# A hybrid decoder layer on one core: x laid out transposed by the host, and the per-layer embedding product put ahead of the normalisation

## The chip, the core and the metric

The kernel runs on one NeuronCore of a Trainium2 chip. A core has a matrix engine (TensorE, PE in the rows; PEld are its weight loads), a vector engine (DVE), a scalar engine (ScalarE, ACT), GpSimd (POOL), and SyncE (SP), whose queue issues all the DMA transfers here. Data lives in SBUF, matmul results in PSUM, which has eight banks of 128 x 512 float32. The engines run side by side, each takes its own instructions in order, and semaphores tie them together. The metric is the time on the device of one execution, in microseconds (us). Numbers that are worked out come from one profiled execution.

## The reference

One decoder layer over a sequence of 1024 tokens with 1024 features, in float32, and a final RMSNorm:

```python
h = rms_norm(x, norm_mix_g)                        # x * rsqrt(mean(x*x) + eps) * g
proj = einsum('bsd,dc->bsc', h, w_in)              # q k v z_a gk_low | cb cc xc z_c | g_a g_c
o = gla_chunked(q, k, v, gk)                       # gated linear attention, chunks of 64
y_a = (rms_norm(o) * silu(z_a)) @ w_branch_a
y_c = (cb * causal_dwconv(cc * xc) * silu(z_c)) @ w_branch_c
merged = sigmoid(g_a + b_ga) * y_a + sigmoid(g_c + b_gc) * y_c
x = x + merged @ w_out
x = x + sigmoid(rms_norm(x, norm_ple_g) @ w_ple_gate) * (p @ w_ple_proj)   # p: 1024 x 256
return rms_norm(x, norm_final_g)
```

The product `p @ w_ple_proj` (p W_pe here) depends on no other step; it is used only at the end.

## The kernel before

**Products.** Each float32 operand is split into a high and a low part: `split` casts to the high part on ScalarE and subtracts on DVE for the low part. A product is then three matmuls (`mm3`: high-high, high-low, low-high). The large products go by a Strassen scheme with seven products instead of eight: a `Cell` is one output block of 256 weight columns by 1024 tokens, and its product `k` (0 to 6) takes four kt of three matmuls of 512 columns, so 12 matmuls. The right side of product `k` is a combination of the four quarters of h, `hres[k]`, made by `build_a`: h0 and h3 are single quarters (`hq0`, `hq3`), both from the first 512 tokens; h1, h2 and h5 need sums of quarters, h4 and h6 need the others. The weights' side is loaded, split and put in a ring for each product.

**Start.** Sixteen warm-up matmuls on a zero tile run first (line 851). The loads in program order are: half the columns of W_pe (`wr_`), half the tokens of p transposed (`pr_`), a small table of vectors (`vec`), four tiles of x of 128 tokens each, the other halves of W_pe and p, and four more tiles of x (lines 864 to 873). One load of W_pe or p is 512 KB, both kt together.

**h.** `prep_x` (line 884) handles one tile of 128 tokens: ScalarE squares it and sums along the row, POOL makes the power -1/2 (`rstd_of`), DVE scales the tile, TensorE transposes eight blocks of 128 x 128 through PSUM, and DVE takes them out with the gain, `hq`.

**p W_pe.** `pe_block(b, c)` (line 897) is one block of 128 tokens by 512 columns: two kt of `mm3`, six matmuls, in one of two PSUM banks (m4, m5), copied out by ScalarE into one of four T buffers and stored to DRAM as `ped` for the end. Sixteen blocks make 96 matmuls. The first eight are among the fixed main order (`nc.side = False`); the later eight (tokens 512 on) are side work, which the planner may put between main matmuls where it likes.

**Early products.** Behind them stand sixteen products (`two_products`, line 914): products 0 and 3 of the eight gate cells, which use h0 and h3 alone. Then the layer goes on: v, q and k, z_a, conv, gates with attention woven in, branch outputs, out, and the last gate.

**Order.** All operations are noted first and put in order by a planner in the file (`Flow`). `set_dues` gives each operation the latest time that its successors allow; `put_in_order` then simulates five engines, taking at each step, among the operations that are ready on an engine, the one due first. The matmuls with `side` false keep program order; everything else is fitted in. A load is taken to have landed `LATE` (2.2 us) after its bytes would have passed at 340 KB per us. A side matmul is not planned before 0.5 us (`SIDE`) after its input from another engine. The result is a fixed order for each engine; the waits themselves are semaphores.

**Places.** Tiles of the long-lived pool `keep` take their place in SBUF when first used in that order (`Buffer.get`).

Of the kernel before, what the change touches and what calls it, by code (L numbers as in the profile page):

```python
# [162 lines left out]
class Pool:  # L163
# [60 lines left out]
class Op:  # L224
    __slots__ = ("n", "engine", "call", "args", "kw", "cost", "lat", "side", "table", "bytes", "name",
                 "preds", "succs", "left", "ready", "due", "start", "bufs")
# [10 lines left out]
class Flow:  # L237
# [5 lines left out]
    def __init__(self, tc):  # L243
        nc = tc.nc
        self.tc, self.ops, self.side, self.open = tc, [], True, []
        self.tensor, self.vector, self.scalar = Port(self, PE, nc.tensor), Port(self, DVE, nc.vector), Port(self, ACT, nc.scalar)
        self.gpsimd, self.sync = Port(self, POOL, nc.gpsimd), Port(self, SP, nc.sync)


    def note(self, engine, op, call, args, kw):  # L250
# [7 lines left out]
        o.side, o.table, o.bytes, o.bufs = self.side, 0, 0, []  # L258
# [114 lines left out]

    def put_in_order(self):
# [28 lines left out]
        while len(order) < len(ops):  # L403
# [36 lines left out]
            for b in o.bufs:  # L440
# [7 lines left out]
                b.until = max(b.until, pipe + LATE if e == SP else when + cost + (0.0 if e == PE and not o.side else o.lat))  # L448
# [5 lines left out]
    def emit(self):  # L454
        self.set_dues()
        place = lambda a: a.place() if isinstance(a, View) else a
        with self.tc.manual_schedule():
            for o in self.put_in_order():
# [7 lines left out]
LATE = 2.2  # L466


@with_exitstack
def kernel(  # L470
# [8 lines left out]
    pT: bass.AP,  # L479
    vecs: bass.AP,  # L480
# [13 lines left out]
    cp = rp = bp = sm = Pool(nc, "keep", Place(tc, "keep"))  # L494
# [19 lines left out]
    junk = cp.tile([P, D], BF16, name="junk")  # L514
# [333 lines left out]
    nc.vector.memset(f(zero), 0.0)  # L848
    warm = [psm.tile([P, 512], F32, tag=f"m{i}", name=f"warm{i}") for i in range(6)]
    nc.side = False  # L850
    for n in range(16):
# [3 lines left out]
    with phase("prep0") as pool:  # L855
        pr_ = slot(4, "h", "pTraw", (2, SEQ), F32)
        wr_ = slot(4, "l", "wperaw", (2, D), F32)
        xs = [slot(1 + n // 2, "hl"[n % 2], f"x0_{n}", (2, D), F32) for n in range(4)]
        xt = [xs[st // 2][:, st % 2, :] for st in range(8)]
# [3 lines left out]

        load(wr_[:, :, halves[0]], wpe[:, :, halves[0]])
        load(pr_[:, :, halves[0]], pT[:, :, halves[0]])
        load(vec, vecs)
        for st in range(4):
            load(xt[st], x[rows(st), :])
        load(wr_[:, :, halves[1]], wpe[:, :, halves[1]])
        load(pr_[:, :, halves[1]], pT[:, :, halves[1]])  # L870
        for st in range(4, 8):
            load(xt[st], x[rows(st), :])
        load(trim, tri)
        pth, ptl = slot(5, "h", "pThi", (2, SEQ)), slot(5, "l", "pTlo", (2, SEQ))
        wph, wpl = slot(6, "h", "wpehi", (2, D)), slot(6, "l", "wpelo", (2, D))

        def split_half(hi, lo, src, hh):
            cs = halves[hh]
            split(hi[:, :, cs], lo[:, :, cs], src[:, :, cs])

        q = [pool.tile([P, 4, HALF], F32, name=f"hq{i}") for i in range(4)]
        quad = {(0, 0): q[0], (1, 0): q[1], (1, 1): q[2], (0, 1): q[3]}

        def prep_x(st):
            ms = sm.tile([P, 1], F32, tag="ms", name=f"ms_x{st}", bufs=4)
            act(junk, xt[st], AF.Square, scale=1.0 / 32.0, accum_out=ms)
            r = rstd_of(ms, f"r_x{st}")
            nc.vector.tensor_scalar(xt[st], xt[st], r[:, 0:1], None, op0=ALU.mult)
            for kh in range(2):
                pt = pso.tile([P, 4, P], F32, tag="o", name=f"pt_x{st}_{kh}", bufs=2)  # L890
                for k in range(4):
                    kk = 4 * kh + k
                    transpose(pt[:, k, :], xt[st][:, kk * P:(kk + 1) * P])
                tt(quad[st // 4, kh][:, :, (st % 4) * P:(st % 4 + 1) * P], pt,
                   gmix[:, 4 * kh:4 * kh + 4, None].to_broadcast([P, 4, P]), op=ALU.mult)

        def pe_block(b, c):
            acc = psm.tile([P, 512], F32, tag=f"m{4 + (b + c) % 2}", name=f"pe{b}_{c}")
            nc.side = b >= 4
            for kt in range(2):  # L900
                mm3(acc, pth[:, kt, rows(b)], ptl[:, kt, rows(b)], wph[:, kt, halves[c]],
                    wpl[:, kt, halves[c]], kt == 0, kt == 1)
            nc.side = True
            t = bp.tile([P, 512], F32, tag="T", name=f"pe{b}_{c}", bufs=4)
            nc.scalar.copy(t, acc)
            store(ped[b][:, halves[c]], t)
# [7 lines left out]
        def two_products(cells):  # L914
            acc = [psm.tile([P, 512], F32, tag=f"m{n}", name=f"{c.name}X") for n, c in enumerate(cells)]
# [9 lines left out]
        split_half(wph, wpl, wr_, 0)  # L925
        split_half(pth, ptl, pr_, 0)
        split_half(wph, wpl, wr_, 1)
        for c in range(2):
            for b in range(4):
                pe_block(b, c)  # L930
        for st in range(4):
            prep_x(st)
        step(0)
        step(3)
        split_half(pth, ptl, pr_, 1)
        for st in range(4, 8):
            prep_x(st)
        two_products(pre[:4])
        for k in (1, 2):
            step(k)  # L940
        two_products(pre[4:])
        step(4)
        for c in range(2):
            for b in range(4, 8):
                pe_block(b, c)
# [596 lines left out]
def _lay_out(inp):  # L1542
# [17 lines left out]
    def quads(m):  # L1560
# [17 lines left out]
        "pT": a["p"][0, 0].T.reshape(2, 128, 1024).transpose(1, 0, 2),  # L1578
        "vecs": vecs,
# [23 lines left out]
```

## Time and profile before

| | us |
|---|---|
| median of 3 runs | 1123.13 (1121.92 to 1124.41) |
| the profiled execution | 1122.77 |
| its span, first to last instruction | 1121.0 |

| engine | busy us | share of the span | instructions |
|---|---|---|---|
| TensorE | 1104.3 | 99% | 5144 |
| DVE | 859.0 | 77% | 1377 |
| ScalarE | 586.7 | 52% | 1094 |
| POOL | 70.5 | 6% | 134 |

A timeline row gives the start from the beginning of the span, the length, the engine, the line (all operations come from one helper, so its line is the same), the operation with the tile that it writes and those that it reads, and in brackets the idle time before it with what ended that time. Lengths of matmuls overlap, since they are pipelined; the distance between two starts is what one costs the stream. The granted TensorE clock was full over the whole span (mean 0.997).

### The profile page before, as it was taken

To read this page: it belongs to the slowest core of one execution; us is meant where nothing else is said; L and a number is where in the kernel's file an instruction comes from. 1 tells how busy PE (TensorE), PEld (TensorE's weight loads), DVE (VectorE), ACT (ScalarE), POOL (GpSimd) and SP (SyncE) were. 2 spreads that over 40 slices of the span, in tenths; PEclk is the share of its full clock that TensorE was granted. 3 is DMA by queue.
4 is the path that set the end of the run, shared out by engine and by line. 5 is a ranking of instruction groups with operands and counts; after the bars stand their busy time and mean duration, and the time that the engine had idled before them with its cause. 6 is when DMAs were issued, how large, how long until landed. Compare 5 with 4: busy or idle time off the path is not lost. (4 is left out here: it accounts for less than half of the span.)

```text
span 1121.0 us, 15465 instructions
## 1 busy us (share of the span) xinstructions
PE 1104.3 (99%) x5144; PEld 915.4 (82%) x5144; DVE 859.0 (77%) x1377; ACT 586.7 (52%) x1094; POOL 70.5 (6%) x134
## 2 busy tenths in 40 slices
PE   8999999999999999999999999999999999999996
PEld 6788888888888888888888888888888888787885
DVE  6986775988885956757748677776999888879686
ACT  7766765655444333433343366766736444467553
POOL 1200000000000000000000021220000000102012
PEclk9999999999999999999999999999999999999998
DMA  9744466978993122121222599998595888778944
GB/s 342 277 168 142 133 194 187 282 231 272 318 336 112 65 85 64 49 95 47 94 57 76 173 293 316 338 294 307 183 331 170 282 263 287 294 236 284 314 163 148
DMA packets 154495, 232.66 MB, mean 208 GB/s; under 512 B 12336, under 2 KB 74032, under 8 KB 151344
## 3 DMA queue, kind: packets, MB, share of 16 engines
q1 hardware_dynamic: 154416, 231.68, 62.6%
q8 instruction: 40, 0.66, 0.2%
q14 instruction: 39, 0.32, 0.1%
HBM read 154.04 MB, written 77.59 MB: 207 GB/s over the span
## 5 line engine op out<-in xcount | busy, mean ns | idle before, releaser
L459 ACT ACTIVATE junk<-x 128x512 bf16<-128x512 f32 (+2 forms) x41 | 28.8, 703 | 21.6 <-DVE x L459 16.3
L459 POOL MEMSET t<- 128x2 f32 x8 | 0.8, 100 | 471.5 <-DVE u L459 271.0
L459 POOL TENSOR_SCALAR rg<-ms 128x1 f32<-128x1 f32 x8 | 8.1, 1007 | 259.7 <-ACT junk L459 259.7
L459 DVE TENSOR_TENSOR wt<-wt 128x512 f32<-128x512 f32 x32 | 21.7, 684 | 0.2
L459 DVE SCALAR_TENSOR_TENSOR u<-t,vec,u 128x1024 f32<-128x1024 f32 x16 | 20.4, 1278 | 0.0
L459 POOL TENSOR_TENSOR or<-or,mhalf 128x1 f32<-128x1 f32 x32 | 19.7, 618 | 2.6
L459 DVE COPY_PREDICATED aT<-trim,X 128x128 f32<-128x128 int32 x32 | 9.6, 300 | 11.1 <-PE X L459 8.6
L459 DVE TENSOR_TENSOR oT<-op,szl 128x256 f32<-128x256 f32 x32 | 13.4, 420 | 5.7 <-PE op L459 1.9
L459 ACT ACTIVATE og<-op,or 128x256 f32<-128x256 f32 x32 | 15.1, 472 | 5.1 <-POOL or L459 3.6
L459 POOL TENSOR_SCALAR or<-oms 128x1 f32<-128x1 f32 x32 | 9.8, 305 | 124.2 <-ACT junk L459 124.0
L459 DVE TENSOR_TENSOR vlo<-pt_v,vhi 128x512 fp32r<-128x512 f32 x16 | 11.0, 688 | 7.0 <-ACT vhi L459 6.9
L459 ACT ACT_TABLE_LOAD x12 | 15.4, 1283 | 0.9 <-PEq L1592 0.7
L459 ACT ACTIVATE junk<-op 128x256 bf16<-128x256 f32 x32 | 12.2, 382 | 6.8 <-PE op L459 5.9
L459 PE MATMUL op<-Sh,qkl 128*128 128x256 f32 x56 | 14.8, 284 | 0.0
L459 PE MATMUL pe<-wpehi,pThi 128*128 128x512 f32 x32 | 13.3, 414 | 1.1 <-ACT pThi L459 1.0
L459 ACT CAST vhi<-pt_v 128x512 fp32r<-128x512 f32 x16 | 9.2, 584 | 9.7 <-PE pt_v L459 8.5
L459 PE MATMUL op<-vl,aTh 128*128 128x256 f32 x64 | 13.9, 289 | 0.0
L459 PE MATMUL pe<-wpehi,pTlo 128*128 128x512 f32 x32 | 13.0, 405 | 0.5 <-DVE pTlo L459 0.5
L459 ACT CAST aTh<-aT 128x128 fp32r<-128x128 f32 x32 | 9.5, 297 | 7.4 <-DVE aT L459 7.2
L459 DVE TENSOR_TENSOR gr<-pt_g,vec 128x512 f32<-128x512 f32 x16 | 10.6, 684 | 3.2 <-DMA gd<-gr 2.4
L459 DVE TENSOR_TENSOR Sl<-S,Sh 128x256 fp32r<-128x256 f32 x28 | 11.8, 421 | 1.6 <-ACT Sh L459 1.3
L459 PEld LDWEIGHTS X<-qkl 128*128 128x128 f32 x64 | 11.3, 189 | 1.9
(3228 smaller groups left out, 4195.1 us busy)
## 6 DMA issues: line engine op xcount, KB each, us to landing
qkl<-qkd SPq DMA_DIRECT2D x32, 320.0 KB, 5.1
x<-in_x_dram SPq DMA_DIRECT2D x16, 512.0 KB, 6.0
wt<-in_wb_dram SPq DMA_DIRECT2D x8, 1024.0 KB, 6.4
wtd<-wt SPq DMA_DIRECT2D x32, 256.0 KB, 4.2
vl<-vd SPq DMA_DIRECT2D x32, 256.0 KB, 5.0
uq<-ud SPq DMA_DIRECT2D x5, 1024.0 KB, 6.6
oq<-od SPq DMA_DIRECT2D x5, 1024.0 KB, 7.0
ped<-pe SPq DMA_DIRECT2D x16, 256.0 KB, 3.1
```

The source lines that it names most:

```text
L459: o.call(*[place(a) for a in o.args], **{k: place(a) for k, a in o.kw.items()})
```

## The change

- The host hands in x a second time, transposed (`xT`), as eight kt of 128 features by 1024 tokens. The four quarters `hq` are loaded from it directly; the eight tiles of x are no longer loaded here, nor transposed.
- `scale_h(i)` takes the place of `prep_x` for one half of the tokens: ScalarE squares the eight kt (four instructions of 1024 columns), DVE adds them up to two, eight float32 matmuls of one column against `ones` sum over the features into PSUM, DVE adds EPS, POOL takes the power -1/2 of four columns, DVE copies it out four times 128 wide, four transposes bring it along the columns, and eight `scalar_tensor_tensor` scale `hq` with the gain.
- All sixteen blocks of p W_pe stand ahead of the early products in the main order, over six banks; the first four go kt by kt. Their copies alternate between ScalarE and DVE. The early products use other banks in turn.
- The loads of W_pe and p are one kt each (256 KB), p and W_pe by turns; these loads and the splits of W_pe and p are due 8 us earlier for the planner (`hurry`).
- In the first 30 us of the plan a load counts as landed 0.8 us after its bytes, not 2.2 us.
- Nine warm-up matmuls instead of sixteen.
- `lay_out` gives the tiles of `keep` their places before the first instruction, `mhalf` first and then from the largest down; `junk` is half as wide.

```diff
+    def lay_out(self, first):
+        tags = sorted(self.tags.values(), key=lambda t: (t.name != first, -t.buffers[0].size * (1 + (t.buffers[0].dtype != BF16))))
+        for t in tags:
+            b = t.buffers[0]
+            for n in range(len(t.free)):
+                if not any(c.real is not None for c in t.buffers):
+                    self.opened().tile([P, b.size], b.dtype, tag=f"{t.name}_{n}", name=f"at_{t.name}_{n}", bufs=1)
...
+        for o in self.ops:
+            o.due -= o.hurry
...
-                q.ready = max(q.ready, (pipe + LATE if e == SP else when + cost + q.preds[n])
+                q.ready = max(q.ready, (pipe + (LATE if when > START else 0.8) if e == SP else when + cost + q.preds[n])
...
+START = 30.0
...
-    for n in range(16):
+    for n in range(9):
         mm(warm[n % 6], zero[:, 0:P], zero, start=True, stop=True)
...
+        q = [pool.tile([P, 4, HALF], F32, name=f"hq{i}") for i in range(4)]
+        quad = [(0, 0), (1, 0), (1, 1), (0, 1)]
...
+        def get_x(i):
+            for n in (0, 3) if i == 0 else (1, 2):
+                for kp in range(0, 4, 2):
+                    kk = 4 * quad[n][1] + kp
+                    load(q[n][:, kp:kp + 2, :], xT[:, kk:kk + 2, halves[i]])
+
+        nc.hurry = 8.0
+        for kt in range(2):
+            load(pr_[:, kt, halves[0]], pT[:, kt, halves[0]])
+            load(wr_[:, kt, halves[0]], wpe[:, kt, halves[0]])
+        for kt in range(2):
+            load(wr_[:, kt, halves[1]], wpe[:, kt, halves[1]])
+        nc.hurry = 0.0
+        get_x(0)
+        load(vec, vecs)
+        for kt in range(2):
+            load(pr_[:, kt, halves[1]], pT[:, kt, halves[1]])
+        get_x(1)
...
+        def scale_h(i):
+            both = (0, 3) if i == 0 else (1, 2)
+            acc = slot(1, "hl"[i], f"sq{i}", (4, 512), F32)
+            for j, (n, kp) in enumerate((n, kp) for n in both for kp in (0, 2)):
+                d = acc[:, 0:2, :] if j == 0 else acc[:, 2:4, :] if j % 2 else slot(2, "hl"[i], f"sr{i}", (4, 512), F32)[:, 0:2, :]
+                act(d, q[n][:, kp:kp + 2, :], AF.Square, scale=1.0 / 32.0)
+                if j:
+                    tt(acc[:, 0:2, :], acc[:, 0:2, :], d, op=ALU.add)
+            sums = pso.tile([P, 4, P], F32, tag="o", name=f"ms{i}", bufs=2)
+            for s in range(4):
+                for kt in range(2):
+                    mm(sums[:, s, 0:1], acc[:, kt, s * P:(s + 1) * P], ones, start=kt == 0, stop=kt == 1)
+            r = sm.tile([P, 4], F32, tag="rx", name=f"r_x{i}", bufs=2)
+            nc.vector.tensor_scalar(r, sums[:, :, 0], EPS, None, op0=ALU.add)
+            nc.gpsimd.tensor_tensor(r, r, mhalf[:, 0:1].to_broadcast([P, 4]), op=ALU.pow)
+            rb = bp.tile([P, 4, P], F32, tag="u2", name=f"rb{i}", bufs=2)
+            nc.vector.tensor_copy(rb, r[:, :, None].to_broadcast([P, 4, P]))
+            rt = pso.tile([P, 4, P], F32, tag="o", name=f"rt{i}", bufs=2)
+            for s in range(4):
+                transpose(rt[:, s, :], rb[:, s, :])
+            rt = rt.rearrange("p s t -> p (s t)")
+            for n in both:
+                for k in range(4):
+                    kk = 4 * quad[n][1] + k
+                    stt(q[n][:, k, :], q[n][:, k, :], gmix[:, kk:kk + 1], rt, op0=ALU.mult, op1=ALU.mult)
+
+        at = [0]
+        BANKS = (0, 1, 2, 3, 4, 5, 0, 1, 2, 3, 4, 5, 0, 1, 2, 3)
+
+        def pe_blocks(bs, c, by_kt=False):
+            acc = []
+            for b in bs:
+                n = BANKS[at[0]] if at[0] < len(BANKS) else 4 + at[0] % 2
+                acc.append(psm.tile([P, 512], F32, tag=f"m{n}", name=f"pe{b}_{c}"))
+                at[0] += 1
+            todo = [(b, kt) for kt in range(2) for b in bs] if by_kt else [(b, kt) for b in bs for kt in range(2)]
+            for b, kt in todo:
+                nc.side = at[0] > len(BANKS)
+                mm3(acc[b - bs[0]], pth[:, kt, rows(b)], ptl[:, kt, rows(b)], wph[:, kt, halves[c]],
                     wpl[:, kt, halves[c]], kt == 0, kt == 1)
+                nc.side = True
+                if kt == 1:
+                    t = bp.tile([P, 512], F32, tag="T", name=f"pe{b}_{c}", bufs=4)
+                    (nc.vector.tensor_copy if b % 2 else nc.scalar.copy)(t, acc[b - bs[0]])
+                    store(ped[b][:, halves[c]], t)
...
+        nc.hurry = 8.0
+        for kt in range(2):
+            split(pth[:, kt, halves[0]], ptl[:, kt, halves[0]], pr_[:, kt, halves[0]])
+            split(wph[:, kt, halves[0]], wpl[:, kt, halves[0]], wr_[:, kt, halves[0]])
+        nc.hurry = 0.0
+        pe_blocks(range(0, 4), 0, True)
         split_half(wph, wpl, wr_, 1)
...
+        pe_blocks(range(0, 4), 1)
+        split_half(pth, ptl, pr_, 1)
+        pe_blocks(range(4, 8), 0)
+        pe_blocks(range(4, 8), 1)
+        scale_h(0)
         step(0)
         step(3)
...
+        two_products(pre[:4], (4, 5, 0, 1))
+        scale_h(1)
         for k in (1, 2):
             step(k)
+        two_products(pre[4:], (2, 3, 4, 5))
         step(4)
```

## Rows read from the trace of the kernel before

**Rows 1.** The page, busy time of each engine: us (share of span) xinstructions.

```profile
PE 1104.3 (99%) x5144; PEld 915.4 (82%) x5144; DVE 859.0 (77%) x1377; ACT 586.7 (52%) x1094; POOL 70.5 (6%) x134
```

**Rows 2.** TensorE waits behind 100 us: us in total, times, longest.

```profile
PE out0V L459 <- ACT out0hi L459: 0.7, 1, 0.7
```

**Rows 3.** Timeline of TensorE near 60 us: start, length, engine, operation, idle before.

```profile
60.19 0.39 PE L459 MATMUL ga3pX<-h3hi,ga3phi 128*128 128x512 f32 x1
60.42 0.39 PE L459 MATMUL ga3pX<-h3lo,ga3phi 128*128 128x512 f32 x1
```

**Rows 4.** Timeline of TensorE, the start.

```profile
1.44 3.78 PE L459 MATMUL warm<-zero 128*128 128x512 f32 x8 [1.44 <-DVE zero L459]
...
8.15 0.50 PE L459 MATMUL pe<-wpehi,pThi 128*128 128x512 f32 x1 [1.03 <-ACT pThi L459]
8.49 0.39 PE L459 MATMUL pe<-wpelo,pThi 128*128 128x512 f32 x1
9.41 0.50 PE L459 MATMUL pe<-wpehi,pTlo 128*128 128x512 f32 x1 [0.53 <-DVE pTlo L459]
```

**Rows 5.** Timeline of TensorE, two later stops and what ended them.

```profile
25.07 0.50 PE L459 MATMUL ga0pX<-h0lo,ga0phi 128*128 128x512 f32 x1 [0.84 <-DVE h0lo L459]
...
34.85 0.66 PE L459 MATMUL pt_x<-ident,x 128*128 128x128 f32 x4 [0.56 <-DVE hq L459]
```

**Rows 6.** First load issue; DMA queue view, 40 slices of the first 40 us.

```profile
0.72 0.69 SPq L459 DMA_DIRECT2D wperaw<-in_wpe_dram  x1
...
GB/s 0 0 223 330 320 311 330 367 401 426 396 396 399 397 399 412 383 369 354 367 373 412 389 401 412 375 315 324 365 385 387 391 334 393 389 318 90 297 279 193
```

**Rows 7.** Timeline of ScalarE, the start.

```profile
4.62 1.05 ACT L459 CAST wpehi<-wperaw 128x1024 fp32r<-128x1024 f32 x1 [2.62 <-DMA wperaw<-in_wpe_dram]
7.05 1.04 ACT L459 CAST pThi<-pTraw 128x1024 fp32r<-128x1024 f32 x1 [1.39 <-DMA pTraw<-in_pT_dram]
...
16.28 0.62 ACT L459 CAST ga0phi<-ga0praw 128x512 fp32r<-128x512 f32 x1
```

**Rows 8.** Timeline of DVE, 26 to 32 us.

```profile
26.07 2.35 DVE L459 TENSOR_TENSOR h3lo<-hq,h3hi 128x1024 fp32r<-128x1024 f32 x2
...
30.15 0.69 DVE L459 TENSOR_TENSOR gc0plo<-gc0praw,gc0phi 128x512 fp32r<-128x512 f32 x1
31.60 0.78 DVE L459 TENSOR_SCALAR x<-x,r_x 128x1024 f32<-128x1024 f32 x1 [0.77 <-POOL r_x L459]
```

**Rows 9.** Timeline of TensorE, four transposes and the next matmuls.

```profile
20.66 0.60 PE L459 MATMUL pt_x<-ident,x 128*128 128x128 f32 x4
21.01 0.47 PE L459 MATMUL pe<-wpehi,pTlo 128*128 128x512 f32 x1
21.32 0.39 PE L459 MATMUL pe<-wpehi,pThi 128*128 128x512 f32 x1
```

**Rows 10.** Timeline of TensorE in the attention stage, a float32 matmul and a transpose.

```profile
646.35 0.38 PE L459 MATMUL X<-qkl 128*128 128x128 f32 x2
646.57 0.27 PE L459 MATMUL X<-ident,qkl 128*128 128x128 f32 x1
646.60 0.48 PE L459 MATMUL ga0V<-h5hi,ga0hi 128*128 128x512 f32 x1
```

**Rows 11.** Windows, 40 to 60 us: busy us (xinstructions) of each engine, granted clock.

```profile
40.00:60.00 20.00, 19.98 (x92) 15.88 (x91) 18.80 (x20) 14.47 (x22) 0.64 (x2) 1.00 0.66 232
```

**Rows 12.** Timeline of POOL, 26 to 32 us.

```profile
27.47 3.44 POOL L459 TENSOR_SCALAR r_x<-ms_x 128x1 f32<-128x1 f32 x1 [10.42 <-ACT junk L459]
31.00 0.57 POOL L459 TENSOR_TENSOR r_x<-r_x,mhalf 128x1 f32<-128x1 f32 x1
```

**Rows 13.** Tile S, one kind: duration ns min/median/max, first and last start.

```profile
L459 DVE SCALAR_TENSOR_TENSOR S<-S,dds,X x24: 471/474/476, 654.9 to 755.8; 128x256 f32<-128x256 f32 x24
```

**Rows 14.** Tensor ped, first 30 us: issues (ns) and landing.

```profile
L459 SPq DMA_DIRECT2D ped<-pe x2: 326/328/330, 11.7 to 13.2; - x2
...
DMA to landing us min/median/max: 4.7/5.1/5.5
```

More of the change, by code (lines that the diff above doesn't have):

```diff
@@ L225 @@
     __slots__ = ("n", "engine", "call", "args", "kw", "cost", "lat", "side", "table", "bytes", "name",
-                 "preds", "succs", "left", "ready", "due", "start", "bufs")
+                 "preds", "succs", "left", "ready", "due", "start", "bufs", "hurry")
 class Port:
@@ L257, in note @@
         o.n, o.engine, o.call, o.args, o.kw = len(self.ops), engine, call, args, kw
-        o.side, o.table, o.bytes, o.bufs = self.side, 0, 0, []
+        o.side, o.table, o.bytes, o.bufs, o.hurry = self.side, 0, 0, [], self.hurry
         label = lambda v: v.buf.name if isinstance(v, View) else "in"
@@ L447, in put_in_order @@
                     b.ends[e] = when + cost
-                b.until = max(b.until, pipe + LATE if e == SP else when + cost + (0.0 if e == PE and not o.side else o.lat))
+                b.until = max(b.until, pipe + (LATE if when > START else 0.8) if e == SP else when + cost + (0.0 if e == PE and not o.side else o.lat))
                 if not b.left:
@@ L456, in emit @@
         place = lambda a: a.place() if isinstance(a, View) else a
+        order = self.put_in_order()
+        self.keep.lay_out("mhalf")
         with self.tc.manual_schedule():
-            for o in self.put_in_order():
+            for o in order:
                 o.call(*[place(a) for a in o.args], **{k: place(a) for k, a in o.kw.items()})
@@ L479 @@
     pT: bass.AP,
+    xT: bass.AP,
     vecs: bass.AP,
@@ L848 @@
     nc.vector.memset(f(zero), 0.0)
+    ones = sm.tile([P, 1], F32, name="ones")
+    nc.gpsimd.memset(ones, 1.0)
     warm = [psm.tile([P, 512], F32, tag=f"m{i}", name=f"warm{i}") for i in range(6)]
     nc.side = False
-    for n in range(16):
+    for n in range(9):
         mm(warm[n % 6], zero[:, 0:P], zero, start=True, stop=True)
@@ L862 @@
                for m, bias, dst in (("ga", bga, gad), ("gc", bgc, gcd)) for c in range(4)]
[L864 to L873, printed above, removed]
+        q = [pool.tile([P, 4, HALF], F32, name=f"hq{i}") for i in range(4)]
@@ L874 @@
+        quad = [(0, 0), (1, 0), (1, 1), (0, 1)]
         pth, ptl = slot(5, "h", "pThi", (2, SEQ)), slot(5, "l", "pTlo", (2, SEQ))
         wph, wpl = slot(6, "h", "wpehi", (2, D)), slot(6, "l", "wpelo", (2, D))
-        def split_half(hi, lo, src, hh):
[L878 to L890, printed above, removed]
-                for k in range(4):
[L892 to L901, printed above, removed]
-                    wpl[:, kt, halves[c]], kt == 0, kt == 1)
[L903 to L906, printed above, removed]
+        def get_x(i):
[3 more added lines that the diff above has]
+                    load(q[n][:, kp:kp + 2, :], xT[:, kk:kk + 2, halves[i]])
@@ new lines @@
+        nc.hurry = 8.0
[10 more added lines that the diff above has]
+        get_x(1)
+        load(trim, tri)
+        def split_half(hi, lo, src, hh):
+            nc.hurry = 8.0
+            for kt in range(2):
+                cs = halves[hh]
+                split(hi[:, kt, cs], lo[:, kt, cs], src[:, kt, cs])
+            nc.hurry = 0.0
@@ L912, in step, with two_products @@
             hres[k] = hb[k]
-        def two_products(cells):
-            acc = [psm.tile([P, 512], F32, tag=f"m{n}", name=f"{c.name}X") for n, c in enumerate(cells)]
+        def two_products(cells, banks):
+            acc = [psm.tile([P, 512], F32, tag=f"m{n}", name=f"{c.name}X") for n, c in zip(banks, cells)]
             for c, X in zip(cells, acc):
@@ L1578, in _lay_out @@
         "pT": a["p"][0, 0].T.reshape(2, 128, 1024).transpose(1, 0, 2),
+        "xT": a["x"][0].T.reshape(8, 128, 1024).transpose(1, 0, 2),
         "vecs": vecs,
```

26 lines of the change are left out of this document (6 added, 20 removed).

## Prediction

> **What bounds the kernel now.** I read the page's busy shares first: TensorE is busy 99% of the span [rows 1]. The reader should see there that shortening other engines buys nothing by itself: the time is TensorE's own instructions plus the places where it stands. So I then read its waits and its timeline. Behind 100 us the longest entry in the list of waits is 0.7 us [rows 2]; in the steady part the product matmuls follow each other every 0.227 us [rows 3]. What the change touches lies ahead of that stream, so the question is how much earlier the stream gets going, and how many instructions leave it.
>
> The start of before: warm-up matmuls from 1.44 us, then idle until pThi, first p W_pe matmul at 8.15 [rows 4]. After it a gap is the distance between two starts less 0.23: 8.49 to 9.41 gives 0.69, where the row itself says 0.53 of idle, so a restart costs 0.16 more than the idle time shown. The two other stops, 0.84 for h0lo and 0.56 for a transpose [rows 5], are then 1.00 and 0.72. Together 2.4 us of standing after 8.15.
>
> **The change, part by part.**
>
> *The first matmul.* Before, ScalarE waits for the first load, 512 KB of W_pe issued at 0.72, until 4.62, and for the second, 512 KB of p, until 7.05; its cast of 1024 columns takes 1.04, and TensorE starts at 8.15 [rows 4, 6, 7]. After, these loads are cut in four of 256 KB, p and W_pe by turns, and the first matmul needs two of them: as many bytes as the one load that had landed by 4.62. A cast of 512 columns takes 0.62 [rows 7], and 0.06 passes between the cast's end at 8.09 and the matmul at 8.15. So 4.62 + 0.62 + 0.06 = 5.30. The warm-up is cut to nine: the first eight take 3.78 us from 1.44 [rows 4], so the ninth ends near 5.5. I take 5.4: 2.75 us earlier (1.9 if the pair lands as late as 5.5; 3.1 if warm-up and landing both let it start at 5.05).
>
> *Its second matmul* needs wpelo, one DVE subtraction of 512 columns, 0.69 [rows 8], behind the cast: a gap of about 0.45. The second kt is needed eleven matmuls later, at 8.4; its two loads land one and two 256 KB transfers later, 0.8 us each at 330 KB per us [rows 6], by 6.2, so its parts are there by 7.6. No stall.
>
> *Work taken from TensorE.* The 64 transposes of x go. Four of them push the stream back by 0.35 (20.66 to 21.01), and the next matmul by 0.31 - 0.23 = 0.08 [rows 9]: 0.43 for four, 16 x 0.43 = 6.9 us, all in the continuous stream and so on the path. New on TensorE: eight transposes of the broadcast rstd, 2 x 0.43 = 0.9; and sixteen float32 matmuls of one column against ones. Nothing in the trace is one column wide. The nearest row is the float32 matmul of 128 columns, which is two instructions, 646.35 to 646.57, 0.11 each [rows 10]; 32 x 0.11 = 3.5, with 0.3 for the stream resumed 3.8. From below, an instruction can start 0.03 behind a transpose (646.57 to 646.60): 32 x 0.03 = 1.0. I take 3.8, because the 128 x 128 to be loaded as weights is the same. Net -6.9 + 0.9 + 3.8 = -2.2 us (to -5.0 with the lower end).
>
> *The order.* All 96 matmuls of p W_pe now run first: 5.4 + 0.45 + 96 x 0.227 = 27.6 us [rows 3], plus the first half's sums and transposes, 2.3: the first product wants h0 at about 30. Moving the blocks costs no TensorE time; but before, the later 48 of them were filler while DVE was busy 18.8 of 20 us [rows 11]. Is that filler missed? The sixteen early products read h0 and h3 alone, both made of the first half of the rows of x, so the second half is not wanted for another 16 x 12 x 0.227 = 43.6 us. In this time DVE has some twelve wlo (12 x 0.69 = 8.3), the second half's three adds (1.18 each, half of 2.35 [rows 8]) and eight scalings (0.74, below), 9.5, and for h3, h1, h2 and h4 about 16 x 1.18 = 19: 37 of 44 us. Cover enough.
>
> *h0 in time.* Six loads of 256 KB and four of 512 KB go ahead of it, 3.7 MB at 330 KB per us from 2.0 us, with 1 us of lag as for the first load: 14.2 us [rows 6, 7]. Then, each from its nearest row: last square 1.05 (as the cast of 1024), add 1.18, 16.4; eight sums 1.8; rstd 0.2 and 0.57 on DVE and POOL [rows 12]; broadcast copy 0.4, four transposes 0.5, 19.9; four scalings (a scalar_tensor_tensor of 256 columns takes 0.47 [rows 13]; 0.27 for 256 more, half of 1.18 - 0.69 and a little, gives 0.74), 22.9; last cast and subtraction 2.2: 25.1. DVE's other work in the stretch (six copies of blocks, two wlo, 0.69 each at most) can push that to 28 or so. Slack 2 to 5 us. Where it gives: the planner lines sums and transposes up between matmuls, and a transpose lined up earlier than its input is there holds TensorE, as at 34.85 [rows 5]. I allow 0.5 for each half and 0.5 at the first product: 1.5 + 0.45 = 1.95 of standing against 2.4, -0.45 (from -1.95 without these to +1.5).
>
> *The rest.* Squares, adds, scalings and casts run on ScalarE and DVE beside TensorE, at nothing while the slack holds. Loads' precedence and the shorter delay in the planner make the first matmul early; counted there. Tiles' places in order of size change addresses alone: the products already stand at 0.227 us, so I book nothing, and within 1 us either way for the later order, which the planner works out anew (nearest row: one late wait of 0.7 [rows 2]).
>
> *Sum.* -2.75 - 2.2 - 0.45 = -5.4. The profiled span of 1121.0 becomes 1115.6; 1.8 lie around it in that execution (1122.77), and the median 1123.13 is 0.36 above that: about **1117.7 us**. With the bounds: 1114.5 to 1120.0.
>
> **Rivals.**
>
> *The loads come no sooner.* If the four 256 KB transfers share the queue and land together, the first pair is there only after 1 MB, when p landed before: cast from 7.05 to 7.67, start at 7.7, a gain of 0.4 instead of 2.75: 1120.0. For it: the second load of before came 2.4 us after the first, not the 1.5 of its bytes. Against it: the first did land by 4.62 with others issued behind it [rows 6, 7].
>
> *POOL held off by DVE.* Each half's rstd has a pow on POOL between DVE steps. At 27.47 a one-column POOL instruction took 3.44, against 0.57 for the pow behind it, while DVE ran subtractions without a pause; it ended at 30.91, when DVE had gone idle [rows 8, 12]. If pow stands like that in both halves, beyond the planner's margin of 0.5, TensorE, in order, stands 2 x (3.44 - 0.57 - 0.5) = 4.7 at the transposes instead of the 1.0 allowed there: 1121.4, no change. Against it: DVE's own broadcast copy waits for pow, so DVE goes idle after at most the few instructions queued between. [...]
>
> *Blocks' copies stand for their buffers: slower.* The sixteen block copies share four T buffers, each freed when its store has landed. Copy 0.62 (as the cast), issue 0.33 and landing 5.1 (the two in the first 30 us took 4.7 and 5.5 [rows 14]) make a turn of 6.05 per four blocks, which TensorE computes in 5.45. Three turns: 1.8 us late, inside the slack. But the copies stand in order on ScalarE and DVE ahead of the squares and scalings of h0, and all filler is spent: at a landing L the chain is late by 3 x (L - 4.5). The gain without the 1.5 allowed is 6.9, the slack about 4: from 10.9 us late, L = 8.1, the kernel is slower than before. At L = 10 it stands 16.5 - 4 = 12.5: 1123.1 - 6.9 + 12.5 = 1128.7. Against it: neither early store took that long.
>
> **How the numbers follow.** Forecast 0.66, 1117.7 (own range 1114.5 to 1120.0, all of it faster). Loads no sooner 0.12, 1120.0, faster. POOL 0.13, 1121.4, no change. T buffers 0.09, slower. A measurement of this kernel can tell about 0.2%, 2.2 us, from no change. So faster 0.78, same 0.13, slower 0.09. The range takes the forecast's bounds, the second case and the third: 1114.3 to 1121.6.
>
> **What would show it.** First p W_pe matmul near 5.4 us; no gap over 0.5 us until the products; the 32 instructions of the sums 0.03 to 0.11 apart; first product near 30 us; behind it the rows of before, 5 us earlier. Wrong, if the first product stands for h0lo by more than 3 us, if ScalarE waits for ped stores, if pow takes over 2 us with TensorE waiting behind it, or if the waits behind 100 us grow.

## The result, and the profile after

The changed kernel takes **1113.45 us** (1113.04 to 1114.01), the one before 1123.77 on the same chip: a ratio of 0.9909 [0.9892, 0.9927]. That is faster, as forecast, but 4.25 us below the forecast of 1117.7 and 0.85 below the range. The executions of before spread from 1121.9 to 1125.2, and its profiled one is among the short ones, so medians gain 10.3 us and profiled executions 8.9 (1122.77 to 1113.84); what follows is accounted in the profiles.

The page of after, span and busy time of each engine, as in [rows 1]:

```profile
span 1112.1 us, 15377 instructions
PE 1098.6 (99%) x5113; PEld 912.6 (82%) x5113; DVE 865.6 (78%) x1391; ACT 582.8 (52%) x1082; POOL 59.5 (5%) x121
```

TensorE's timeline in after: the start, the first half's sums and transposes, and the first products. It answers to [rows 4, 5, 9].

```profile
1.44 4.21 PE L474 MATMUL warm<-zero 128*128 128x512 f32 x9 [1.44 <-DVE zero L474]
5.45 0.71 PE L474 MATMUL pe<-wpehi,pThi 128*128 128x512 f32 x1
5.95 0.63 PE L474 MATMUL pe<-wpelo,pThi 128*128 128x512 f32 x1
6.38 0.63 PE L474 MATMUL pe<-wpehi,pTlo 128*128 128x512 f32 x1
6.80 0.45 PE L474 MATMUL pe<-wpehi,pThi 128*128 128x512 f32 x1
7.09 0.39 PE L474 MATMUL pe<-wpelo,pThi 128*128 128x512 f32 x1
...
19.10 1.84 PE L474 MATMUL ms<-ones,sq 128*128 128x1 f32 x16
20.80 0.49 PE L474 MATMUL pe<-wpehi,pThi 128*128 128x512 f32 x1
21.13 0.40 PE L474 MATMUL pe<-wpelo,pThi 128*128 128x512 f32 x1
...
23.22 0.60 PE L474 MATMUL rt<-ident,rb 128*128 128x128 f32 x4
23.58 0.48 PE L474 MATMUL pe<-wpelo,pThi 128*128 128x512 f32 x1
23.90 0.39 PE L474 MATMUL pe<-wpehi,pTlo 128*128 128x512 f32 x1
...
30.27 0.39 PE L474 MATMUL ga0pX<-h0hi,ga0phi 128*128 128x512 f32 x1
...
31.86 0.39 PE L474 MATMUL ga0pX<-h0lo,ga0phi 128*128 128x512 f32 x1
```

There is no idle time in brackets after 1.44 us: the stops of before between 8 and 35 us have no successor. One of them [rows 5] does not show, since its idle time is short; the distance is 0.51, so 0.29 too much:

```profile
32.01 0.39 PE L459 MATMUL ga2pX<-h0lo,ga2phi 128*128 128x512 f32 x1
32.52 1.06 PE L459 MATMUL pt_x<-ident,x 128*128 128x128 f32 x8
```

Three other things are to be seen in after. The first matmuls stand 0.50, 0.43, 0.42 and 0.29 apart, about double the usual distance at first. Sixteen one-column instructions take 20.80 - 19.10 = 1.70 us. And behind the sums the matmuls stand 0.23 apart for a while, where they stood 0.227 before them.

What fed TensorE in after: ScalarE's first casts and one copy of a block, DVE's second half of h0lo, and POOL's two powers.

```profile
4.03 0.62 ACT L474 CAST wpehi<-wperaw 128x512 fp32r<-128x512 f32 x1 [2.03 <-DMA wperaw<-in_wpe_dram]
4.68 0.62 ACT L474 CAST pThi<-pTraw 128x512 fp32r<-128x512 f32 x1
...
17.80 0.59 ACT L474 COPY pe<-pe 128x512 f32<-128x512 f32 x1 [0.35 <-DMA ped<-pe]
```

```profile
22.67 0.43 DVE L474 COPY rb<-r_x 128x512 f32<-128x512 f32 x1 [0.92 <-POOL r_x L474]
...
29.18 1.21 DVE L474 TENSOR_TENSOR h0lo<-hq,h0hi 128x1024 fp32r<-128x1024 f32 x1
```

```profile
21.30 1.34 POOL L474 TENSOR_TENSOR r_x<-r_x,mhalf 128x4 f32<-128x4 f32 x1 [19.98 <-DVE r_x L474]
47.12 1.02 POOL L474 TENSOR_TENSOR r_x<-r_x,mhalf 128x4 f32<-128x4 f32 x1 [24.48 <-DVE r_x L474]
```

**The account.** A fixed mark is the first q product, behind all that was changed; its rows in before and in after:

```profile
178.00 0.39 PE L459 MATMUL q0X<-h0hi,q0hi 128*128 128x512 f32 x1
```

```profile
168.81 0.39 PE L474 MATMUL q0X<-h0hi,q0hi 128*128 128x512 f32 x1
```

So 9.2 us are gained ahead of it (0.3 are lost behind it). A second profile of each kernel has 177.53 and 168.43, so the mark moves by some 0.4 us from one execution to the next. Distances between TensorE's starts, after less before, summed by what stands there:

| us | |
|---|---|
| first block earlier, 8.15 to 5.45 | -2.7 |
| 64 transposes of x | -6.1 |
| 32 instructions of the sums | +3.4 |
| eight transposes of rstd | +0.7 |
| stops of before that are gone (0.69, 1.01, 0.29, 0.73, and 0.24 at 106 us) | -2.9 |
| first matmuls at double distance | +0.7 |
| the rest: the first matmul behind a stop or a group of transposes, 0.31 to 0.34 instead of 0.227; gaps of up to 0.2 between products; 0.1 in all for matmuls at 0.229 to 0.237 | -2.3 |

### The profile page after: what moved, and what is told of

It is laid out like the page before. It is cut to its first block, busy times and chain, and to the rows that moved or that the text cites. A ratio compares the mean times of both kernels' runs of the same rounds, so it can differ in the third digit from the quotient of the medians.

```text
span 1112.1 us, 15377 instructions
## 1 busy us (share of the span) xinstructions
PE 1098.6 (99%) x5113; PEld 912.6 (82%) x5113; DVE 865.6 (78%) x1391; ACT 582.8 (52%) x1082; POOL 59.5 (5%) x121
## 4 chain that ended last, share of the span: by engine, by line
PE 93%; DVE 3%; DMA 2%; issue 1%; ACT 0%; POOL 0%; SPq 0%; POOLq 0%; DVEq 0%; ACTq 0%
PE op L474 2%; PE pe L474 2%; PE X L474 2%; DMA qkl<-qkd 1%; PE ga2Y L474 1%; PE ga3Y L474 1%; PE gc1Y L474 1%; PE gc0Y L474 1%; PE v2Y L474 1%; PE gt0Y L474 1%; PE v1Y L474 1%; PE v3Y L474 1%; PE v0Y L474 1%; PE out3Y L474 1%; PE out0Y L474 1%; PE gt1Y L474 1%
## 5 line engine op out<-in xcount | busy, mean ns | idle before, releaser
L474 ACT ACTIVATE junk<-x 128x512 bf16<-128x512 f32 (+1 forms) x33 | 20.3, 616 | 20.6 <-DVE x L474 15.6
L474 PE MATMUL X<-qkl 128*128 128x128 f32 x64 | 12.5, 276 | 0.7 <-DMA qkl<-qkd 0.5
L474 PE MATMUL X<-vl,keh 128*128 128x256 f32 x56 | 12.9, 312 | 0.0
L474 PE MATMUL pe<-wpelo,pThi 128*128 128x512 f32 x32 | 12.8, 400 | 0.0
```

The source lines that it names most:

```text
L474: o.call(*[place(a) for a in o.args], **{k: place(a) for k, a in o.kw.items()})
```

## The experiments

The open question was where the unforeseen 3.5 us of the profiles came from: out of the work removed (a transpose costs more than its own time: the first matmul behind a group stands 0.31 instead of 0.227 [rows 9]) or out of the order (the early blocks cover what TensorE used to stand for). Edits are to the changed kernel unless said otherwise.

**The changed kernel again**, and the p W_pe part alone: blocks, loads, planner and places as changed, x as in before (`prep_x` with its 64 transposes).

> The changed kernel again, beside the runs that it is compared with. Theory S (the stream's own account): of 9.2 us that the changed kernel is ahead when the q products begin, 2.7 are the earlier first matmul, 2.9 stops of TensorE that are gone, 2.7 transposes less sums, and about 0.9 slower matmuls behind each break. It gives 1113 to 1114 us, 0.991 of before. Theory F (the forecast's terms, 5.4 us) gives 1118.

> The other part alone: blocks first over six banks, cut loads with precedence, nine warm-up matmuls, planner and places as changed; x still loaded in tiles, scaled and transposed on TensorE. S: the earlier first matmul (2.7) and some of the stops (1 to 2.5) go, the 64 transposes stay: 3.5 to 5.5 us ahead of before, 1118.5 to 1120.5 us. R: everything but the 2.7 of transposes, 6.5 us ahead, 1117. A missing filler (h0 late, blocks all spent): the first product stands for h0lo by several us and the kernel is no faster than before.

They took 1113.62, ratio 0.9888 [0.9868, 0.9908], and 1116.13, 0.9908 [0.9888, 0.9928], beside 1125.83 for before. The x part adds 2.5 us only. The second kernel came out better than theory S had it, and nearer to R. With the transposes still in it, the second kernel has no stop between 1.44 us and its first q product:

```profile
171.78 0.39 PE L474 MATMUL q0X<-h0hi,q0hi 128*128 128x512 f32 x1
```

That is 6.2 us ahead of before, of which the start explains 2.5 (its first block stands at 5.68). So it is the order over six banks, with the start, that took the stops away.

**The later eight blocks as side work behind the products again**, over two banks.

```diff
-        pe_blocks(range(4, 8), 0)
-        pe_blocks(range(4, 8), 1)
         scale_h(0)
...
         step(4)
+        pe_blocks(range(4, 8), 0)
+        pe_blocks(range(4, 8), 1)
```

> The changed kernel with the later eight blocks of p W_pe put back as filler behind the early products (two banks, side work), everything else as changed. If the filler is not missed (forecast and S): h0 is then wanted 11 us earlier, near 19 us, and can't be there before 28: TensorE stands some 6 to 9 us at the first product, or the planner pulls the blocks forward and nothing changes; 1113 to 1122. If moving the blocks was worth nothing: 1113 to 1114, and the blocks stand ahead of the first product anyway.

It took 1125.38, ratio 1.0 [0.9985, 1.0015]: 11.8 us over the changed kernel, the whole gain, and more than either expectation. Its timeline of TensorE:

```profile
17.21 0.50 PE L474 MATMUL pe<-wpehi,pThi 128*128 128x512 f32 x1 [2.89 <-ACT pe L474]
...
28.05 0.51 PE L474 MATMUL ga0pX<-h0hi,ga0phi 128*128 128x512 f32 x1 [2.57 <-ACT h0hi L474]
...
29.43 0.79 PE L474 MATMUL ga0pX<-h0lo,ga0phi 128*128 128x512 f32 x1 [0.87 <-DVE h0lo L474]
```

TensorE stands 6.3 us in three stops: the first for one of the two banks, which ScalarE's late copy frees, the other two for h0, with no block left to do meanwhile. The stops are not the whole price. Behind the first one the granted clock falls (in a window, the third number from the end; here 0.50), and matmuls stand 0.43 apart:

```profile
20.00:25.00 5.00, 5.00 (x15) 4.02 (x16) 3.00 (x6) 1.66 (x3) 1.34 (x1) 0.50 1.06 381
```

At the first q product (181.22) this kernel is 12.4 us behind the changed one: 6.9 in the stops with their restarts, 4.8 at the lower clock. The edit puts back the two banks together with the old order, and no run takes them apart, so what the order is worth without the banks is not shown.

**The x part alone** on the kernel before, tiles placed by first use as there.

> The x part alone on the kernel before: x loaded transposed and scaled in place; order, loads of p and W_pe, warm-up and planner as before. S: 2.7 us of transposes less sums, the stops at 32 to 34 us (1.0 us) and most of the slower matmuls go, the first matmul stays near 8.2: 4 to 5.5 us ahead of before, 1118 to 1120 us. F: 2.2 us of work alone, 1121. Rival R (the surplus of 3.8 us over the forecast comes from the planner's new order and the tiles' places): at most 2.7 us, 1121.

1139.96, ratio 1.0122 [1.0098, 1.0147]: much slower, which nothing in any of my reasons explained. The products stood 0.230 to 0.232 apart in every stage. The places of tiles came under suspicion; see the runs on places below.

**The start: uncut loads, the old plan, sixteen warm-ups.** First, the first half of p and all of W_pe in loads of 512 KB, W_pe first:

```diff
-        for kt in range(2):
-            load(pr_[:, kt, halves[0]], pT[:, kt, halves[0]])
-            load(wr_[:, kt, halves[0]], wpe[:, kt, halves[0]])
+        load(wr_[:, :, halves[0]], wpe[:, :, halves[0]])
+        load(pr_[:, :, halves[0]], pT[:, :, halves[0]])
...
```

> The changed kernel with W_pe and p loaded 512 KB at a time, W_pe first, as before. S: the first matmul falls back to 7.5 to 8.2 us, 2 to 2.7 us slower than the changed kernel. If h0 is what sets the first product at 30 us: 0 to 0.5 slower.

1117.35, ratio 0.9937 [0.992, 0.9953], 3.7 us over the changed kernel. TensorE's first block there:

```profile
8.61 0.59 PE L474 MATMUL pe<-wpehi,pThi 128*128 128x512 f32 x1 [2.98 <-ACT pThi L474]
```

Again the clock falls behind the stop, so not all of the 3.7 is the later start (3.2 in the profile):

```profile
9.00:10.00 1.00, 1.00 (x4) 0.57 (x3) 0.97 (x3) 0.82 (x3) 0.00 (x0) 0.50 1.02 383
```

Second, no precedence and the long delay in the plan (`START = -1.0`, `o.due -= 0.0`):

> The changed kernel without the planner's part: no 8 us of precedence for the loads and splits of p and W_pe, and a load counted as landed 2.2 us after its bytes also in the first 30 us. S: places of a few instructions differ; if precedence is what makes the first matmul early, loads of x go ahead and it starts 0.5 to 2.5 us later (1114 to 1116). R: most of the surplus of 3.8 us is lost, 1117.

1114.2, 0.9913 [0.9898, 0.9927], first block at 5.55. So the loads, cut and by turns, make the first matmul early, and the planner's two edits are worth nothing that shows. Third, `range(16)` for the warm-ups:

> The changed kernel with sixteen warm-up matmuls instead of nine. In the changed kernel the first three p W_pe matmuls are 0.43 to 0.50 us apart, twice the later distance. With sixteen, the warm-up ends near 7.1 us instead of 5.4, and the first matmuls run at 0.23: 1.1 us slower if the slow matmuls are gone with it, 1.7 if not. If the early start is worth less than it looks (h0 sets the first product anyway): no slower.

1114.22, 0.9913 [0.9898, 0.9927]: 0.6 more than the changed kernel's 1113.62 on another chip; in the profiles its first q product is 1.1 later (169.92). The first block waits until 7.31, and no matmul then stands at double distance. But with nine warm-ups that happens too; the second profile of the changed kernel:

```profile
5.36 0.50 PE L474 MATMUL pe<-wpehi,pThi 128*128 128x512 f32 x1
5.70 0.40 PE L474 MATMUL pe<-wpelo,pThi 128*128 128x512 f32 x1
6.08 0.51 PE L474 MATMUL pe<-wpehi,pTlo 128*128 128x512 f32 x1
6.43 0.40 PE L474 MATMUL pe<-wpehi,pThi 128*128 128x512 f32 x1
```

So nine warm-ups don't bring the double distance by themselves; it differs from one execution to the next. The clock's row has 1.00 in both, but the trace of after holds no record of the clock before 6.91 us, where the double distance ends, and the second one none before 4.94; 0.43 is the distance that the run with uncut loads shows at a granted clock of 0.50.

**Work on TensorE.** Four unread transposes behind each block put the 64 back, and nothing else; then the sums with their two kt added on DVE first, 8 instead of 16 matmuls:

```diff
+            tt(acc[:, 0, :], acc[:, 0, :], acc[:, 1, :], op=ALU.add)
             for s in range(4):
-                for kt in range(2):
-                    mm(sums[:, s, 0:1], acc[:, kt, s * P:(s + 1) * P], ones, start=kt == 0, stop=kt == 1)
+                mm(sums[:, s, 0:1], acc[:, 0, s * P:(s + 1) * P], ones, start=True, stop=True)
```

> The changed kernel with 64 transposes of 128 x 128 put in again, four behind each block of p W_pe, with nothing reading them: what they cost by themselves. The forecast's price: 16 x 0.43 = 6.9 us slower. S: 7.2 for the transposes and the matmul behind each group, and matmuls at 0.230 to 0.232 instead of 0.227 for some twenty behind each: 7.5 to 8.3. Less than 5 if part of them was hidden.

> The changed kernel with the two remaining kt of the squares added on DVE, so that eight one-column float32 matmuls do instead of sixteen. S: 16 instructions less, 1.7 us faster, at 0.6 us of DVE in each half: 1111.5 to 1112.5.

The first took 1121.01, ratio 0.9969 [0.9957, 0.9982], 7.4 more than the changed kernel, and its first q product is 7.36 later: 5.67 in the transposes, 1.23 in the block matmuls behind them, the rest in products. The forecast had 6.9. Its timeline, one group of four:

```profile
11.34 0.39 PE L474 MATMUL pe<-wpehi,pTlo 128*128 128x512 f32 x1
11.57 0.60 PE L474 MATMUL pt_d<-ident 128*128 128x128 f32 x4
11.92 0.48 PE L474 MATMUL pe<-wpehi,pThi 128*128 128x512 f32 x1
12.24 0.39 PE L474 MATMUL pe<-wpelo,pThi 128*128 128x512 f32 x1
```

The second took **1112.03**, ratio 0.9881 [0.9866, 0.9896]: 1.6 less than the changed kernel's 1113.62 on another chip, the fastest of all. Eight instructions in place of sixteen take 0.81 us instead of 1.70 (its own rows), and DVE's added operation hides:

```profile
19.92 0.95 PE L474 MATMUL ms<-ones,sq 128*128 128x1 f32 x8
20.73 0.48 PE L474 MATMUL pe<-wpehi,pTlo 128*128 128x512 f32 x1
```

**The sums twice**: a second pair of the same matmuls into a column that nobody reads.

> The changed kernel with the sixteen one-column float32 matmuls made twice (the second time into a column that nobody reads): 32 instructions more on TensorE, and rstd later by 1.7 us in each half. By the trace of after, 16 take 1.70 us: 3.4 us slower, plus what h0 then comes late: h0lo's second half was there at 30.3, when the first product began at 30.27, so up to 1.7 more if the stream does not move with it. By the forecast's lower bound (0.03 each): 1.0.

1122.18, ratio 0.9982 [0.9971, 0.9994]: 8.6 more, where the instructions themselves cost 4.8 and the expectation was at most 5.1 (its profile, at 1124.50, is longer than its median). Its windows (start:end, length, busy us with instructions of TensorE, its loads, DVE, ScalarE, POOL, then granted clock) and its timeline behind the first sums:

```profile
20.00:30.00 10.00, 10.00 (x43) 8.54 (x43) 4.07 (x9) 2.87 (x6) 1.34 (x1) 0.66 0.88 292
50.00:60.00 10.00, 10.00 (x45) 8.62 (x46) 3.39 (x7) 1.21 (x2) 1.41 (x1) 0.66 0.55 201
```

```profile
18.66 4.39 PE L474 MATMUL ms<-ones,sq 128*128 128x1 f32 x32
22.91 0.77 PE L474 MATMUL pe<-wpehi,pThi 128*128 128x512 f32 x1
23.48 0.63 PE L474 MATMUL pe<-wpelo,pThi 128*128 128x512 f32 x1
23.91 0.63 PE L474 MATMUL pe<-wpehi,pTlo 128*128 128x512 f32 x1
```

The 32 instructions of one column took 4.25 (18.66 to 22.91), not twice 1.70; the granted clock was 0.66 in the mean of each of those windows, and matmuls behind them stood 0.43 apart, as at 0.50 in the run with the late blocks. Block and product matmuls together are 4.7 us longer than in after, most of it here. Around sixteen in a row, in the changed kernel, the clock's row has 1.00.

**Three buffers for the copies of blocks** instead of four (`t = ev(f"pe{b}_{c}")`), for the third rival.

> The changed kernel with the block copies going through three buffers (shared with the early products' copies) instead of four. By the forecast's rival of the copies: a turn of 6.05 us per three blocks, which TensorE computes in 4.1, so the chain is 5 x 1.95 = 10 us late and TensorE stands 5 to 10 us: 1118 to 1124. If stores land faster than 5.1 us: under 2 us.

1117.46, ratio 0.9937 [0.9922, 0.9951]: 3.8 more. Its profile, of the longest of four executions (1120.20), has two stops that cost 1.0 and 1.7, and a granted clock of 0.51 between 45 and 50 us behind the second. Both stops wait for DVE, for a copy of a block and for an addition; the longest wait of a copy for a store is one of 0.43 on ScalarE. So fewer buffers cost time, in a plan that comes out differently, but the wait for stores that the rival is about isn't seen.

**Places.** First, the changed kernel without `lay_out`:

```diff
-        self.keep.lay_out("mhalf")
```

> The changed kernel with the tiles' places taken in order of first use, as before. S and the forecast: addresses cost nothing, within 0.5 us of the changed kernel, product matmuls 0.227 us apart. R: 1 to 4 us slower.

1131.77, ratio 1.0065 [1.0049, 1.0082]: 18 us over the changed kernel. Its first product starts at 30.01, as early as in the changed one; its products then stand 0.230 to 0.232 apart to the end. Listed from the built kernels, all places in `keep` are multiples of 32 bytes, and TensorE's large operands start at 32 modulo 64 in before and after; in this one and in the x part alone they are mixed, since the tile `ones`, one column wide, pushes what is placed behind it by 32 bytes. The theory formed then: what counts is whether the two operands of a matmul start alike modulo 64. A pad of one column in front of everything big (all at 0), against a pad behind the resident tiles, in front of the streamed weights (weights at 0, h at 32):

```diff
+                    if t.name == first:
+                        self.opened().tile([P, 1], F32, tag="pada", name="at_pada", bufs=1)
```

```diff
+                    if t.name == "u2" and n == 0:
+                        self.opened().tile([P, 1], F32, tag="pada", name="at_pada", bufs=1)
```

> The changed kernel with every large tile moved by 32 bytes, so that all operands of TensorE start on a multiple of 64. Theory U (the mixture of starts is what costs): as the changed kernel, 1113 to 1114.5, matmuls 0.227 us apart. Theory V (a start on a multiple of 64 is the slow one): 0.231 or more and 1131 us or above. Theory W (the sizes' order itself, which puts neighbours together, is what helps, not the start): 1113.5.

> The changed kernel with the resident operand (h, u, o, the weights of the last stages) 32 bytes past a multiple of 64 and the ring of the other operand on it. U: mixed between the two operands of one matmul, 0.231, 1130 us; if only a mixture from one matmul to the next costs: 1113.5. V: half of the reads slow, 1120 to 1130. W: 1113.5.

1113.73, ratio 0.9903 [0.9888, 0.9918], against 1138.8, 1.0127 [1.0112, 1.0142]. Windows of 100 us in the middle, the first of all shifted, the second of weights shifted:

```profile
400.00:500.00 100.00, 100.00 (x443) 82.84 (x442) 61.48 (x91) 37.95 (x66) 0.20 (x2) 1.00 0.21 67
```

```profile
400.00:500.00 100.00, 100.00 (x430) 80.51 (x429) 62.13 (x93) 34.56 (x60) 0.20 (x2) 1.00 0.23 75
```

Same work, busy 100% and clock 1.00 in both, and 3% fewer matmuls done in the second. Both operands at 0 or both at 32 gives 0.227 a product matmul, one of each 0.233; over some 4400 of them that makes the difference of 25 us. U had named 1130, near the run without places; but there only about half of the matmuls have operands that differ. With the starts listed beside each matmul, the trace of that run agrees: 0.233 where they differ, 0.229 to 0.231 where they are alike (why not 0.227 stays open). In the changed kernel itself 32 matmuls have operands that differ, and they stand 0.234 apart.

**The x part alone with the places laid out:**

> The x part alone on the kernel before, now with the tiles' places in order of size, so that all operands of TensorE start alike. By the trace of the run without places, where the products were 0.231 to 0.232 us apart over the whole span (4400 x 0.0045 = 20 us): 1139.9 - 20 = 1120 us. By the difference between the changed kernel and the run of the other part alone (2.5 us): 1121.

1121.93, ratio 0.9983 [0.9967, 0.9999]; the 18 us of the run without places are gone, but there is no gain ahead of the first q product (178.24). Three stops of TensorE, on the pe banks and on h0, and a granted clock of 0.76 between 25 and 30 us behind them, ate the transposes' time:

```profile
15.76 0.50 PE L471 MATMUL pe<-wpehi,pThi 128*128 128x512 f32 x1 [1.20 <-ACT pe L471]
...
24.96 0.50 PE L471 MATMUL ga0pX<-h0hi,ga0phi 128*128 128x512 f32 x1 [1.14 <-ACT h0hi L471]
...
26.33 0.50 PE L471 MATMUL ga0pX<-h0lo,ga0phi 128*128 128x512 f32 x1 [0.87 <-DVE h0lo L471]
```

**The start alone and the order alone**, both on the kernel before with places laid out: cut loads and nine warm-ups; all sixteen blocks first over six banks.

> The kernel before with the first loads cut in 256 KB, p and W_pe by turns, and nine warm-up matmuls; blocks in the order of before; tiles' places as in the changed kernel. The first matmul comes 2.5 us earlier, but h0 is ready when it was (25 us), so the early start should turn into a longer stop before the first product: 0 to 1 us ahead of before. If an early start is worth its time anywhere: 2.5.

> The kernel before with all sixteen blocks of p W_pe ahead of h over six banks, and nothing else of the change but the tiles' places (operands start alike). If the order removes the stops: the 1.0 us for h0lo, the 0.3 and 0.7 at 32 to 34 us and the small ones go, the first matmul stays at 8.2, 64 transposes stay: 2.5 to 4 us ahead of before. If the stops go with the early start: 0 to 1.

1121.93, 0.9973 [0.9958, 0.9987], and 1120.83, 0.9964 [0.9947, 0.9981]. At the first q product the start alone is 1.0 us ahead of before, the order alone 2.8, both together (the p W_pe part) 6.2. With the old order the early start turns into stops, first for the second kt of p, then at h0:

```profile
7.37 0.50 PE L471 MATMUL pe<-wpehi,pThi 128*128 128x512 f32 x1 [0.84 <-ACT pThi L471]
...
25.11 0.50 PE L471 MATMUL ga0pX<-h0lo,ga0phi 128*128 128x512 f32 x1 [1.43 <-DVE h0lo L471]
```

**The kernel before again**, for the spread of its times.

> The kernel before, profiled once more. Its runs spread over 4 us (1122 to 1126), those of the changed kernel over 1.3. If its start is what differs (stops at the hand-over from the blocks to h0, or a clock that falls in them): the difference to the first profile lies in the first 100 us. If not: it is spread over the span, or lies in the late waits at 950 to 1035 us.

1121.73, span 1120.0, with the same stops, all some 0.4 us earlier. It is a short one again, so a long one was not caught. But each execution has its mean granted clock on record. Of 65 executions of before beside the other runs (one of 2314 us left out), the 31 at 0.997 or more have a median of 1123.4 us, the 15 at 0.995 or less one of 1126.3; the changed kernel's eight are all at 0.997 or 0.998. So the longer ones go with a lower clock. That it falls behind the stops, as in the runs above, fits, but isn't shown.

## Why the prediction was right in sign and too small

**First matmul: right.** 5.45 for 5.4; cast at 4.03, the second at 4.68. Its inner reason was half wrong: precedence and delay in the plan, which I counted in, are worth nothing that shows; the loads, cut and by turns, do it alone.

**The gap for wpelo: wrong in kind, small.** No gap of 0.45; instead four matmuls at up to double distance, 0.74 in all; that a lower clock made them isn't shown. In the second profile it is 0.39, and the first distances there are 0.34, 0.38 and 0.35. I had priced the start at 0.227, which neither profile has for these first matmuls.

**Work: right.** Sums 1.70 for sixteen instructions, 0.106 each, 3.6 with the restarts for 3.8; rstd's transposes 0.9 with theirs, as forecast; the 64 transposes 7.4 for 6.9. Net -2.9 for -2.2.

**Standing: the step that failed.** I set 2.4 us of standing before against 1.95 after, -0.45. Measured: 2.9 of stops gone (0.5 of them not in my 2.4: those at 32.5 and 106 us) and none new, 0.74 for the slow first matmuls, and 1.4 for the first matmuls behind stops, gaps between products and matmuls at 0.229 to 0.237 (the account's 2.3 less the restarts that I count with the transposes and sums): 2.9 + 1.4 - 0.74 = 3.6 instead of 0.45. Two errors of size in it. The 1.5 that I allowed for sums, transposes and the first product did not occur: each had its input in time. And a stop costs more than the distance at its own place: behind the one that ends at 25.07 in before, the first matmul takes 0.34, 0.11 too much, and the next six 0.229 to 0.236, together 0.03 too much; I had read 0.227 off at 60 us, where nothing had broken the stream since 54.5. With the work's 0.7, the 3.1 here makes 3.8; 0.3 are given back later: the 3.5 by which the profiles missed. The other 0.75 of 4.25 is how medians stand to profiles: +0.36 in before, -0.39 in after. The range was too narrow by its own terms, too: the lower bounds of the three terms, -3.1, -5.0 and -1.95, make 1113.1 and not 1114.5. That the result lies within this is luck, for the standing is outside its own bound, and the work far from its lower one.

**The order: rightly not missed as filler, wrongly worth nothing.** I asked only whether moving the later blocks would hurt. Moving them, over six banks, is what removes the stops: put back, with two banks, 11.8 us are lost, about 7 in stops and about 5 at the granted clock of 0.50 behind them. The parts don't add up either: start and order are worth 1.0 and 2.8 alone and 6.2 together, the x part nothing alone and 3.0 on top. My sum assumed that each edit keeps its worth without the others.

**h0 in time: barely.** DVE's second half of h0lo ends at 29.18 + 1.21 = 30.39, not at 25 to 28, and the first product that reads it starts at 31.86: 1.5 us of slack, not 2 to 5. The last square began 15.92, where I had the loads done by 14.2, and DVE put other work between the steps. The forecast of the first product, about 30, was right: 30.27.

**Rivals.** Loads no sooner: refuted by 4.03 and 4.68. POOL held off: the powers took 1.34 and 1.02, more than [rows 12]'s 0.57 but not 3.44, and DVE's copy of rstd waited 0.92 for the first; TensorE had blocks to do meanwhile and did not stand. The first power, from 21.30, began while DVE ran a subtraction (21.06, 0.69 long). The second ran while DVE was idle (from 47.04 to 48.17), so four columns took 1.02 with nothing on DVE, and the first took 0.3 more; that the subtraction held it off for these 0.3 is my estimate, which no run tests. T buffers: ScalarE waited once, 0.35, one of my own signs of being wrong, and TensorE did not stand for it; with three buffers the kernel is 3.8 slower, though not by waits for stores.

**Places: right in the sum, wrong as a step.** Before and after both have operands that start alike, so the net is nothing. But "change addresses alone" was wrong: without `lay_out` the same change is slower than before by 0.65%. Before owed its 0.227 to the order in which tiles happened to be used first. A rival that I should have named, since the change adds a tile of one column: 18 us.

## What to carry to other kernels

When TensorE is the bound, price an order by whether the stream ever breaks: here a stop cost its gap, 0.14 us in the matmuls behind it (25.07 in before), and with the late blocks 4.8 us at a granted clock of 0.50; the start alone, its first block 2.85 us earlier, was worth 1.0, as the next waits took the rest. Test the parts of a change together and apart, since a gain in one place can turn into a stop at the next. And compare the distance of the steady matmuls before and after any edit that adds a tile, however small: here one column, with tiles placed by first use, took it from 0.227 to 0.230 and more.

## What the runs showed of the hardware that I had not expected

- A product matmul cost 0.227 us where its two operands start alike modulo 64 bytes (all shifted, 1113.73 us) and 0.233 where they don't (weights shifted, 1138.8 us), with TensorE 100% busy and the clock at 1.00 in both; in the windows of 100 us the count of matmuls tells them apart, 443 against 430.
- The first matmul behind a stop or a group of four transposes stands 0.31 to 0.34 us ahead of the next one (0.34 at 25.07 in before, 0.32 at 23.58 in after); at these two, six and five more at 0.228 to 0.236 follow before 0.227 is back.
- Around the end of 32 float32 matmul instructions of one column in a row, 4.25 us, the granted clock was 0.66 in the mean of 10 us (the sums twice, 20 to 30 us), with TensorE busy for all 10.00; around sixteen it was 1.00 (after, 18 to 24 us).
- Behind some stops of TensorE the granted clock was lower: 0.50 behind 2.98 us (uncut loads, 9 to 10 us) and behind 2.89 us (late blocks, 20 to 25 us), with matmuls 0.43 apart, eight in a row in the second; behind the stops of before, at most 1.03 us, it was 1.00.
